# A four-layer hybrid decoder trunk on one core: wide value projection, split conditioning, transposes put later, inverse joins set apart, residual stream kept by blocks

## The chip, the core and the metric

The kernel runs on one core of a Trainium2 chip. The metric is the device time of one execution in microseconds, the median of several. TensorE (PE) multiplies matrices, and its weight loads (PEld) overlap its matmuls; VectorE (DVE), ScalarE (ACT) and GpSimd (POOL) work elementwise; SyncE (SP) here only issues DMAs. Each engine runs its instructions in a fixed order.

## What is computed

Four layers work on x of 1024 positions by 1024 features in float32. Each is a norm, a conditioning (shift, scale and gate from a vector c), an input projection, a mixer, a SiLU gate, an output projection and a gated residual add:

```python
for i in range(4):
    mod = c @ ada_w[i] + ada_b[i]                 # 1024 x 3072
    shift, scale, gate = split(mod, 3)
    h = rmsnorm(x, norm_g[i]) * (1 + scale) + shift
    y = (hgrn2, swa, gdn)[i % 3](h)               # layers 0 and 3: hgrn2
    x = x + gate * y
```

- HGRN2 (layers 0 and 3), 8 heads of 128: q, f, values i and gate z are h @ w_in. A gated linear recurrence runs in its chunked form; its output is normed per head, multiplied by silu(z) and projected.
- Attention with a sliding window of 128 (layer 1), 16 query heads, 4 key/value heads, rotary embedding, norms of q and k, learned sinks.
- Gated DeltaNet (layer 2), 8 q/k heads and 16 value heads of 128: a convolution of 4 taps over q, k and v, decays per head, chunks solved with a triangular inverse.

## The kernel before, in words

**Tiles.** x and h are held transposed, features on the 128 partitions. The 1024 positions are two halves of 512 (`hf` 0 and 1); a half is 8 blocks of 128 features. A product in float32 precision is three matmuls in a faster form (`mm3`, L204 to L206): both factors are split into a rounded part `hi` and the rest `lo`, and hi·hi, hi·lo and lo·hi are added. So a weight is loaded as `w_raw` (SP), rounded by ScalarE (`w_hi`, L179) and subtracted by VectorE (`w_lo`, L180). There are three buffers of `raw` and four of each split part.

**Projections.** `proj_fm` (L508) keeps 128 columns of weights in the array and streams 512 positions, for each half 8 blocks x 3 matmuls; then an `evac` function takes the sum from PSUM. `proj_tm` keeps activations in the array and streams 256 columns of weights: the values of HGRN2 (two heads at a time) and q, k and v of the attention layer are made so.

**Start.** `load_x` (L293) transposes a half of x on TensorE. `ada_first` (L389) makes the first four of the six conditioning parts (512 columns each; parts 0 and 1 are the shift, 2 and 3 the scale): 8 matmuls of one row per part on TensorE (L400), and its columns through L449. The norm (`norm_stats`, L467; `norm_apply`, L496) follows, per block of 128 features n_t on VectorE (L504), hhi on ScalarE (L505), hlo on VectorE (L506).

**Conditioning of later layers.** `ada` multiplies on VectorE (L413), one step per block of weights, in pieces that are handed out beside the heads (`take(side, ns)`, `NS` steps per head).

**Weaving.** `weave` interleaves streams of instructions by their estimated costs: beside a head's mixing (`mix`, or `scan` and `inverse` in DeltaNet) go the projections of the next head and the conditioning. A scheduler then fixes each engine's order by priorities; `burst` and `tied` raise the priority of a group of matmuls and keep it together.

**HGRN2's head** (`mix`, L1025). Three steps of levels (1, 3, 5) make the products inside blocks of 2, 8 and 32 positions and, in the last, between the four blocks of 32 of a chunk of 128 (L1087, `lev_ps`, the 32-step). POOL copies the diagonal blocks (L1081). Chunk by chunk come the output `o_ps` and the state. The output is normed (L1132), transposed on TensorE (L1136, `ot_ps`), multiplied by the gate `zs` and stored to `od`; the last head's stays in SBUF.

**DeltaNet.** `conv` (L637) evacuates a projection and runs three steps on VectorE (L650) and two on ScalarE. Its result is transposed on TensorE at once (`trans`, L654: `ktr_ps`, `qtr_ps`, `vtr_ps`). `inverse` solves 16 chunks of 128 positions for two heads; its last part joins blocks of 32 by four small groups of matmuls (`z_ps`, L811 to L836). `ZL` says beside which head the gate projections `proj_z` stand.

**Residual stream.** After each layer x is updated in SBUF block by block (L534, L1216). Its two tiles are needed by the mixers of layers 1 and 2, so there x is stored to `xd` (`spill_x`, one DMA of 2 MB per half) and read back (`fill_x`, the same) ahead of the output projection. In the HGRN2 layers x stays in SBUF.

## Time and profile before

| what | value |
|---|---|
| three runs, us | 2686.42, 2691.14, 2692.78; median 2691.14 |
| profiled execution, its own time | 2695.95 us |
| its span, first to last instruction | 2694.2 us |
| mean granted TensorE clock | 0.992 |
| TensorE, VectorE, ScalarE, POOL busy | 97%, 75%, 47%, 5% |
| moved by DMA | 273.29 MB, mean 101 GB/s |
| chain that ended last: PE, DVE, DMA, ACT | 71%, 17%, 5%, 3% |

The page's groups give a line, an engine, an operation, output<-inputs, the shape, a count, the busy time in us and the mean ns of one, and behind the bar the idle time of the engine ahead of them with what ended it. A row of the timeline gives a start, a duration, the instruction, a count and in brackets the idle time. A row of stretches gives busy time and count for each engine, then the granted clock, the DMA share and GB/s. The stages in the span: start to about 60 us, layer 0 to 640, attention to 1130, DeltaNet to 2130, the second HGRN2 layer to the end.

### The profile page before, as it was taken

The page shows a single profiled execution, that of the slowest core. Times are in us where ns is not written, and L with a number is a line of the kernel's source. Part 1 is how long each engine was busy: PE and PEld are TensorE (multiplying, and loading weights), DVE is VectorE, ACT ScalarE, POOL GpSimd, SP SyncE. Part 2 cuts the span into 40 slices and gives each one's busy share as a digit, 9 for nine tenths or more (in the row PEclk, how much of TensorE's full clock was granted, in tenths as well). Part 3 has the DMA queues.
Part 4 walks back from the last instruction along what each step waited for, and adds up shares of the span by engine and source line. Part 5 has one row for each costly group of instructions (what it writes and reads, how often), then busy time and mean ns, then how long its engine had stood idle before and what let it go on. Part 6 is the DMA issues. An engine that isn't in the chain of part 4 may idle for free.

```text
span 2694.2 us, 51458 instructions
## 1 busy us (share of the span) xinstructions
PE 2609.7 (97%) x18927; PEld 2102.4 (78%) x18927; DVE 2010.2 (75%) x5619; ACT 1272.9 (47%) x3268; POOL 136.7 (5%) x352
## 2 busy tenths in 40 slices
PE   8999999999999999999999999999999999999998
PEld 4878878778878777677877777777788878787877
DVE  6776766788687877777988888989876766656575
ACT  4333333444454655454556556666644433333342
POOL 0000100000000000001001101100000000000000
PEclk9999999999999999999999999999999999999999
DMA  6332222344223252333343333333584221111133
GB/s 241 92 93 84 68 79 72 110 137 157 59 87 103 75 158 91 114 98 84 102 115 99 96 105 100 94 97 82 179 254 132 71 60 37 56 51 43 49 118 115
DMA packets 361490, 273.29 MB, mean 101 GB/s; under 512 B 70499, under 2 KB 294166, under 8 KB 361238
## 3 DMA queue, kind: packets, MB, share of 16 engines
q1 hardware_dynamic: 360950, 268.96, 33.9%
q8 instruction: 149, 2.44, 0.4%
q14 instruction: 103, 0.84, 0.1%
q0 software_dynamic: 288, 1.05, 0.1%
HBM read 224.77 MB, written 45.15 MB: 100 GB/s over the span
## 4 chain that ended last, share of the span: by engine, by line
PE 71%; DVE 17%; DMA 5%; ACT 3%; issue 3%; SPq 1%; POOL 0%; DVEq 0%; ACTq 0%; POOLq 0%
PE proj_ps L206 10%; PE proj_ps L205 9%; PE proj_ps L204 9%; PE outp_ps L204 5%; PE outp_ps L205 5%; PE outp_ps L206 5%; DMA ada_w<-in_ada_w_dram 3%; PE projt_ps L204 3%; PE projt_ps L206 3%; PE projt_ps L205 3%; DVE w_lo L180 2%; DVE gd_tb L650 2%; PE pv_ps L1374 1%; DVE ada_acc L413 1%; PE w_ps L890 1%
## 5 line engine op out<-in xcount | busy, mean ns | idle before, releaser
L204 PE MATMUL proj_ps<-hhi,w_hi 128*128 128x512 f32 x1664 | 675.8, 406 | 6.1 <-ACT gd_tb L648 5.9
L206 PE MATMUL proj_ps<-hhi,w_lo 128*128 128x512 f32 x1664 | 679.9, 409 | 0.0
L205 PE MATMUL proj_ps<-hlo,w_hi 128*128 128x512 f32 x1664 | 671.2, 403 | 0.0
L204 PEld LDWEIGHTS proj_ps<-hhi,w_hi 128*128 128x128 f32 x1664 | 315.3, 190 | 59.4 <-ACT gd_tb L648 6.3
L205 PEld LDWEIGHTS proj_ps<-hlo,w_hi 128*128 128x128 f32 x1664 | 314.7, 189 | 59.0 <-issue 2.4
L206 PEld LDWEIGHTS proj_ps<-hhi,w_lo 128*128 128x128 f32 x1664 | 315.0, 189 | 56.1 <-issue 1.0
L179 ACT CAST w_hi<-w_raw 128x512 fp32r<-128x512 f32 x332 | 202.0, 611 | 303.3 <-PE proj_ps L205 188.1
L180 DVE TENSOR_TENSOR w_lo<-w_raw,w_hi 128x512 fp32r<-128x512 f32 x332 | 223.1, 674 | 155.2 <-ACT w_hi L179 129.1
L205 PE MATMUL projt_ps<-w_lo,hhi 128*128 128x256 f32 x896 | 258.7, 291 | 4.7 <-DVE w_lo L180 4.7
L204 PE MATMUL projt_ps<-w_hi,hhi 128*128 128x256 f32 x896 | 257.8, 290 | 0.6 <-ACT w_hi L179 0.6
L206 PE MATMUL projt_ps<-w_hi,hlo 128*128 128x256 f32 x896 | 256.8, 290 | 0.0
L204 PE MATMUL outp_ps<-o_hi,w_hi 128*128 128x512 f32 x576 | 229.2, 400 | 4.7 <-ACT o_hi L1200 3.4
L205 PE MATMUL outp_ps<-o_lo,w_hi 128*128 128x512 f32 x576 | 229.4, 399 | 0.0
L206 PE MATMUL outp_ps<-o_hi,w_lo 128*128 128x512 f32 x576 | 226.8, 396 | 0.7 <-DVE w_lo L183 0.7
L205 PEld LDWEIGHTS projt_ps<-w_lo,hhi 128*128 128x128 f32 x896 | 171.1, 192 | 8.1 <-DVE w_lo L180 6.0
L204 PEld LDWEIGHTS projt_ps<-w_hi,hhi 128*128 128x128 f32 x896 | 171.1, 192 | 3.7 <-ACT w_hi L179 1.0
L206 PEld LDWEIGHTS projt_ps<-w_hi,hlo 128*128 128x128 f32 x896 | 170.8, 192 | 2.4 <-issue 1.0
L650 DVE SCALAR_TENSOR_TENSOR gd_tb<-gd_xs,taps,gd_tb 128x512 f32<-128x512 f32 x192 | 145.2, 756 | 28.3 <-ACT gd_tb L648 19.7
L182 ACT ACTIVATE w_hi<-w_raw,par 128x512 fp32r<-128x512 f32 (+1 forms) x136 | 94.3, 698 | 137.0 <-PE outp_ps L205 89.2
L204 PEld LDWEIGHTS outp_ps<-o_hi,w_hi 128*128 128x128 f32 x576 | 108.8, 189 | 29.1 <-ACT o_hi L1200 4.9
L413 DVE SCALAR_TENSOR_TENSOR ada_acc<-ada_w,par,ada_acc 128x512 f32<-128x512 f32 x140 | 104.8, 749 | 33.4 <-DMA ada_w<-in_ada_w_dram 32.5
L206 PEld LDWEIGHTS outp_ps<-o_hi,w_lo 128*128 128x128 f32 x576 | 108.7, 189 | 23.5 <-DVE w_lo L183 1.3
(398 smaller groups left out, 4894.8 us busy)
## 6 DMA issues: line engine op xcount, KB each, us to landing
ada_w<-in_ada_w_dram SPq DMA_DIRECT2D x160, 256.0 KB, 2.8
w_raw<-in_hg_in_w_dram SPq DMA_DIRECT2D x136, 256.0 KB, 2.8
w_raw<-in_gd_in_w_dram SPq DMA_DIRECT2D x108, 256.0 KB, 3.0
o_in<-od SPq DMA_DIRECT2D x72, 256.0 KB, 3.2
w_raw<-in_gd_out_w_dram SPq DMA_DIRECT2D x64, 256.0 KB, 2.9
w_raw<-in_sw_in_w_dram SPq DMA_DIRECT2D x48, 256.0 KB, 2.9
w_raw<-in_hg_out_w_dram SPq DMA_DIRECT2D x40, 256.0 KB, 2.8
ada_w<-in_ada_w_dram SPq DMA_DIRECT2D x8, 1024.0 KB, 9.2
```

Of the source, the lines that this page charges most:

```text
L179: nc.scalar.copy(hi, raw)
L180: nc.vector.tensor_tensor(lo, raw, hi.bitcast(F32), ALU.subtract)
L182: nc.scalar.activation(hi, raw, AF.Copy, scale=scale)
L204: mm(out, a[0], b[0], start=start, stop=False)
L205: mm(out, a[0], b[1], start=False, stop=False)
L206: mm(out, a[1], b[0], start=False, stop=stop)
L413: self.nc.vector.scalar_tensor_tensor(acc, w, c, acc, ALU.mult, ALU.add)
L650: nc.vector.scalar_tensor_tensor(y, xs[:, j:j + HT], w(j), y, ALU.mult, ALU.add)
L890: nc.tensor.matmul(po[:, hd[a]], dd["u"][a, hf][:, cs], rhs, start=True, stop=True)
L1374: nc.tensor.matmul(po[a * 64:(a + 1) * 64], vg[:, n + 1 - nkb + b, :], p4[:, :, a, :], start=b == 0, stop=b == nkb - 1)
```

## The change

- **Wide values.** HGRN2's values are made four heads at a time: 512 columns of weights are streamed, eight split weights are held, four of them in buffers of the layer (`load_wide`, `proj_wide`). Values of heads 0 to 6 of a half live in a tile of x, so x is stored and read back in these layers too; head 7 has tiles of its own.
- **Split conditioning, shift on VectorE.** The four first parts are requested at once, the second half of x after them. Parts 2 and 3 (scale) go through TensorE, parts 0 and 1 (shift) through VectorE. After parts 2 and 0 the first four blocks are normed, after 3 and 1 the others. The rotary tables move beside layer 0's heads, and `NS` is 11 for the HGRN2 layers.
- **Output of HGRN2.** For heads 0 to 6 VectorE transposes blocks of 32x32, four DMAs store them to `pd` with the blocks in their places, and during the next half head the whole is read back, multiplied by the gate and stored to `od` (`gate`). The 32-step runs as four groups of columns. The diagonal copies are on ScalarE.
- **Later transposes.** In DeltaNet `evac` may return a function that `proj_fm` runs in the middle of the next sum (`turns`).
- **Joins apart.** The four groups of joins are put behind the last projection matmul then issued (`apart`), and the inverse has a higher estimated cost.
- **Norm in pieces.** The second half's norm of a layer is handed to the next layer (`self.last`); in DeltaNet four blocks are normed behind each convolution, while eight projections of the first half run.
- **Residual by blocks.** Each finished block of x is stored from POOL's queue (`keep_x`) and read back ahead of its use in `out_mm`.
- **Gates handed out anew.** DeltaNet's gate projections stand half by half (`ZL`), HGRN2's one head later.
- **Attention** starts with values and half of q, makes all keys in one pass, and ties a block's four products with the values.

```diff
-NS = 8, 16, 10
-ZL = ((2, 0, 1),), ((3, 0, 1),), ((4, 0, 1),), ((5, 0, 1),), ((6, 0),), ((6, 1),), ((7, 0, 1),), ()
+NS = 11, 16, 10
+ZL = ((2, 1), (3, 0)), ((3, 1),), ((4, 0),), ((4, 1), (5, 0)), ((5, 1),), ((6, 0),), ((6, 1), (7, 0, 1)), ()
...
+    def keep_x(self, hf, j):
+        if self.more:
+            x, d = self.block(hf, j)
+            self.nc.gpsimd.dma_start(d, x)
...
+    def apart(self, mms):
+        with self.tc.issue_after(self.mm.ins):
+            self.tied(mms)
...
+    def load_wide(self, w, c0, pool):
+        return [self.load_w(w[:, k, c0:c0 + HT], None, (None, pool)[k % 2]) for k in range(KT)]
...
     def ada_step(self, acc, w, k):
...
-            self.nc.vector.scalar_tensor_tensor(acc, w, c, acc, ALU.mult, ALU.add)
+            self.step = self.nc.vector.scalar_tensor_tensor(acc, w, c, acc, ALU.mult, ALU.add)
...
         for k in range(KT):
-            t = self.np.tile([P, HT], F32, name="n_t", tag="n_t", bufs=NB["n_t"])
+            t = self.psum("lev", "n_t", 2)
...
+            yield 1
...
     def proj_fm(self, w, c0, evac, halves=(0, 1)):
...
+                if k == 3:
+                    self.turns()
             with self.tc.high_priority(offset=self.pe):
-                evac(hf, ps)
+                self.turn = evac(hf, ps)
...
             for j in (2, 1, 0):
-                nc.vector.scalar_tensor_tensor(y, xs[:, j:j + HT], w(j), y, ALU.mult, ALU.add)
+                last = nc.vector.scalar_tensor_tensor(y, xs[:, j:j + HT], w(j), y, ALU.mult, ALU.add)
+            self.piece = None
+            with self.tc.issue_after(last.ins):
+                drain(take(self.last, self.parts))
+            self.hold = self.piece
...
-        self.early(proj_kq(0, ds[0], ((0,),)), EV)
-        self.spill_x(1)
+        self.parts = 4
+        self.early(chain(proj_kq(0, ds[0], ((0,),)), proj_z(1, ds[1], (0,)), proj_z(2, ds[2], (0,))), EV)
+        drain(self.last)
...
+        def proj_v(m):
+            def ev(tt, ps):
+                hf, c = divmod(tt, NC)
+                if vs[hf] is None:
+                    vs[hf] = self.xslot("hg_v").rearrange("p (c a) n -> p c (a n)", a=2)
+                n = HT - m * P
+                nc.scalar.copy(vs[hf][:, c, m * HT:m * HT + n], ps[:, :n])
+                if m:
+                    nc.scalar.copy(v7[hf][:, c, :], ps[:, n:])
+            yield from self.proj_wide(self.load_wide(w_in, 2 * D + m * HT, mp), ev, range(2 * NC))
...
+        def gate():
+            h, hf, z = pend.pop()
+            rows = (slice(h * P, (h + 1) * P), slice(hf * HT, (hf + 1) * HT))
+            t = tl("tmp")
+            nc.sync.dma_start(t, self.pd[rows])
+            nc.vector.tensor_tensor(v4(z, "c b"), v4(t, "b c"), v4(z, "c b"), ALU.mult)
+            nc.sync.dma_start(od[rows], z)
...
-                            nc.gpsimd.tensor_copy(at[gs, :, gs], A[gs].rearrange("p (c t) -> p c t", c=NC))
+                            nc.scalar.copy(at[gs, :, gs], A[gs].rearrange("p (c t) -> p c t", c=NC))
...
+                        self.tied([lambda c=c, m=m: mm(c, *m) for c in range(NC) for m in (
+                            (0, 3, slice(6, 7), slice(3, 4)), (0, 0, slice(0, 4, 3), slice(1, 3)),
+                            (1, 1, slice(1, 5, 3), slice(2, 4)), (2, 2, slice(2, 3), slice(3, 4)))])
...
                 if h < HA:
-                    nc.sync.dma_start(od[h * P:(h + 1) * P, hf * HT:(hf + 1) * HT], of)
+                    nc.vector.tensor_tensor(v4(on, "b c"), v4(po, "c b"), r[:, :, None, None].to_broadcast([P, NC, 4, 32]), ALU.mult)
+                    ob = tl("tmp")
+                    nc.vector.transpose(ob, on)
...
+                    for a in range(4):
+                        nc.sync.dma_start(dst[a], ob[a * 32:(a + 1) * 32].rearrange("q (b t) -> q b t", b=4))
+                    pend.append((h, hf, d["zs", hf]))
...
+            gs = {0: [(0, "z")], 1: [], H - 2: [(h, "z"), (h + 1, "qfz")]}.get(h, [(h, "z")])
+            if h < H - 2:
+                gs.append((h + 1, "qfz" if h == 0 else "qf"))
...
+            if (hf, j) in self.due:
+                self.due.remove((hf, j))
+                self.nc.sync.dma_start(*self.block(hf, j))
...
+        self.early(chain(proj_v(0), proj_q(0, ds[0], (0, 1))))
+        drain(proj_v(1))
+        drain(self.proj_tm(self.load_tm(w_in, 1024), ev_k))
+        drain(chain(proj_z(0, ds[0]), proj_q(0, ds[0], (2, 3))))
...
+        for part, bank, col in ((2, ("lev", "ada_row", 2), 0), (0, None, D), (3, ("s", "ada_row", 1), None), (1, None, None)):
```

Three places show how the order of instructions moves. First TensorE's order at the start, before (`ada_row` is a conditioning part, the number its weight tile; `ada_ps` its columns, `x_ps` transposes of x, `proj_ps` the first projections):

```order
L400 MATMUL ada_row<-ada_w_362,par 1x512 x7
L400 MATMUL ada_row<-ada_w_383,par 1x512
L449 MATMUL ada_ps<-ones,ada_acc 128x1 x4
L400 MATMUL ada_row<-ada_w_383,par 1x512 x7
L310 MATMUL x_ps<-ident,x_in 128x128 x9
L449 MATMUL ada_ps<-ones,ada_acc 128x1 x4
L310 MATMUL x_ps<-ident,x_in 128x128 x23
L265 MATMUL taps_ps<-ident,taps_in 128x128
L204 MATMUL proj_ps<-hhi,w_hi 128x512
```

And TensorE's order there now:

```order
L331 MATMUL x_ps<-ident,x_in 128x128 x32
L433 MATMUL ada_row<-ada_w_150,par 1x512 x3
L526 MATMUL n_rb<-n_sq,ones 128x512
L433 MATMUL ada_row<-ada_w_150,par 1x512 x5
L485 MATMUL ada_ps<-ones,ada_acc 128x1 x4
L433 MATMUL ada_row<-ada_w_182,par 1x512
L485 MATMUL ada_ps<-ones,ada_acc 128x1 x4
L433 MATMUL ada_row<-ada_w_182,par 1x512
L223 MATMUL proj_ps<-hhi,w_hi 128x512
```

The first projections stood behind all four parts and both halves of x; now 24 of them stand behind part 2, the columns of parts 2 and 0 and two matmuls of part 3, ahead of the second half of x.

Second, VectorE's order at DeltaNet's start, before (`n_t` and `hlo` are the norm of the second half, `gd_tb` the convolution of the first):

```order
L504 SCALAR_TENSOR_TENSOR n_t<-x_11280,gcol,n_rb 128x512 x2
L180 TENSOR_TENSOR w_lo<-w_raw,w_hi 128x512
L506 SCALAR_TENSOR_TENSOR hlo<-n_t,mod,hhi 128x512 x2
L504 SCALAR_TENSOR_TENSOR n_t<-x_11280,gcol,n_rb 128x512 x2
L180 TENSOR_TENSOR w_lo<-w_raw,w_hi 128x512
L506 SCALAR_TENSOR_TENSOR hlo<-n_t,mod,hhi 128x512 x2
L650 SCALAR_TENSOR_TENSOR gd_tb<-gd_xs,taps,gd_tb 128x512 x2
L556 TENSOR_TENSOR gd_wab<-w_raw,gd_wab 128x8x32
L650 SCALAR_TENSOR_TENSOR gd_tb<-gd_xs,taps,gd_tb 128x512
```

And VectorE's order there now:

```order
L695 SCALAR_TENSOR_TENSOR gd_tb<-gd_xs,taps,gd_tb 128x512
L600 TENSOR_TENSOR gd_wab<-w_raw,gd_wab 128x8x32
L695 SCALAR_TENSOR_TENSOR gd_tb<-gd_xs,taps,gd_tb 128x512
L195 TENSOR_TENSOR w_lo<-w_raw,w_hi 128x512
L695 SCALAR_TENSOR_TENSOR gd_tb<-gd_xs,taps,gd_tb 128x512
L538 SCALAR_TENSOR_TENSOR n_t<-x_11000,gcol,n_rb 128x512 x2
L702 SCALAR_TENSOR_TENSOR gd_k<-gd_tb 128x512
L540 SCALAR_TENSOR_TENSOR hlo<-n_t,mod,hhi 128x512 x2
```

The convolution of k stood behind the whole norm of the second half; now the norm's pieces stand behind its three steps.

Third, SP's order in layer 0, before (`ada_w` is conditioning, `od` the outputs of a head):

```order
L177 DMA w_raw<-in_hg_in_w_dram 128x4x128 x2
L427 DMA ada_w<-in_ada_w_dram 128x512 x3
L1141 DMA od_76<-hg_tmp 128x512
L427 DMA ada_w<-in_ada_w_dram 128x512 x2
L177 DMA w_raw<-in_hg_in_w_dram 128x4x128 x2
```

And SP's order there now:

```order
L463 DMA ada_w<-in_ada_w_dram 128x512
L1221 DMA pd<-hg_tmp 32x4x128 x4
L463 DMA ada_w<-in_ada_w_dram 128x512 x3
L1100 DMA hg_tmp<-pd 128x512
L463 DMA ada_w<-in_ada_w_dram 128x512
L192 DMA w_raw<-in_hg_in_w_dram 128x4x128 x2
L1102 DMA od_76<-hg_zs 128x512
L463 DMA ada_w<-in_ada_w_dram 128x512 x3
```

One store became four stores, a read-back and a store, with loads of conditioning and weights between them.

421 lines of the change are left out of this document (240 added, 181 removed).

## The prediction

> **What bounds the kernel now.** I read the busy shares first, then the stretches by stage, then TensorE's groups and what ended its idle time.
>
> ```profile
> PE 2609.7 (97%) x18927; PEld 2102.4 (78%) x18927; DVE 2010.2 (75%) x5619; ACT 1272.9 (47%) x3268; POOL 136.7 (5%) x352
> 60.00:530.00 470.00, 456.73 (x4266) 377.91 (x4266) 330.99 (x1042) 168.25 (x398) 30.81 (x65) 0.99 0.29 85
> 1140.00:1930.00 790.00, 768.66 (x5359) 613.09 (x5357) 670.39 (x1883) 471.56 (x1471) 65.69 (x161) 0.99 0.38 100
> 2130.00:2580.00 450.00, 445.46 (x4241) 372.47 (x4241) 286.95 (x968) 163.71 (x389) 29.10 (x64) 1.00 0.16 48
> ```
>
> The stretches are the first HGRN2 layer, DeltaNet's body and the second HGRN2 layer; the columns are length, then PE, PEld, DVE, ACT, POOL, clock, DMA share, GB/s. TensorE works in 97% of the span and is idle for 2694.2 - 2609.7 = 84.5 us. So the time falls by what the change takes off TensorE's own list, plus idle time that it closes; work added to VectorE or ScalarE costs only where TensorE comes to wait for it. VectorE is the next limit: 670.4 of 790 us in DeltaNet's body.
>
> A matmul's recorded duration overlaps the next one, so I price by start-to-start distances on TensorE's timeline (start, duration):
>
> ```profile
> 66.88 0.39 PE L205 MATMUL proj_ps<-hlo,w_hi 128*128 128x512 f32 x1
> 67.10 0.39 PE L206 MATMUL proj_ps<-hhi,w_lo 128*128 128x512 f32 x1
> 67.33 0.28 PE L204 MATMUL projt_ps<-w_hi,hhi 128*128 128x256 f32 x1
> 67.44 0.28 PE L205 MATMUL projt_ps<-w_lo,hhi 128*128 128x256 f32 x1
> 67.56 0.28 PE L206 MATMUL projt_ps<-w_hi,hlo 128*128 128x256 f32 x1
> 67.68 0.28 PE L204 MATMUL projt_ps<-w_hi,hhi 128*128 128x256 f32 x1
> ```
>
> 512 columns take 0.228 us, 256 take 0.12.
>
> **The change part by part.** Durations are of the profiled execution: span 2694.2, its own time 2695.95 us, 4.8 above the median 2691.1.
>
> *Wide values.* Per HGRN2 layer 768 matmuls of 256 columns become 384 of 512. Both layers: 1536 x 0.12 = 184 against 768 x 0.228 = 175: -9 us. The Trainium skill (TensorE: Matmul & The Clock Gate, "Wait — 56ns, not 53.3ns?") gives N/2.4 ns plus about 2.5 ns for a warm matmul; by that the pairing saves 768 x 2.5 ns = 2 us instead of 9, an estimate from that page. The rows' difference, 2 x 0.12 - 0.228 = 0.012 us, is larger than the page's, and I keep it. Eight split weights are now held through a whole pass, so the next projection's weights get buffers only as the last token tile runs; no row shows this. At each of four passes it costs between nothing and two splits on VectorE (0.69 each, below): 0 to 5 us, taken +2.
>
> *HGRN2 outputs shifted by 32x32 blocks on VectorE.* For seven of eight heads the TensorE transposes go.
>
> ```profile
> 303.48 0.60 PE L1136 MATMUL ot_ps<-ident,hg_tmp 128*128 128x128 f32 x4
> 303.91 0.39 PE L1114 MATMUL o_ps<-hg_S,hg_qf 128*128 128x128 f32 x2
> L1136 PE MATMUL ot_ps<-ident,hg_tmp 128*128 128x128 f32 x128 | 20.8, 280 | 5.9 <-DVE hg_tmp L1132 5.6
> L859 DVE STREAM_TRANSPOSE gd_of<-gd_of 128x512 f32<-128x512 f32 x32 | 22.5, 704 | 0.1
> L1081 POOL COPY hg_at<-hg_A 32x128 f32<-32x128 f32 x128 | 59.9, 468 | 940.3 <-DVE hg_F L1093 556.9 <-DVE hg_A L1076 360.9 <-DVE hg_F L1098 16.8
> ```
>
> Four take 303.91 - 303.48 = 0.43 us, so 28 groups 12.0 us; with 28/32 of the 5.6 us that TensorE waited for their input, -17 us. In their place stand 28 VectorE transposes (0.70 each in DeltaNet's row), a store in four pieces, a read-back and a later gate product. Nothing on TensorE waits for these but the final projection. The 128 copies of the diagonal blocks go from POOL to ScalarE: even at POOL's 0.47 that is 30 us a layer, and ScalarE has worked 168.3 of 470: 0; if its queue is in the way, one copy for each of 32 steps, 15 us.
>
> *The 32-step of the levels.* It now runs 32 records in four column groups, the widest 64, instead of 24 in three with the widest 96.
>
> ```profile
> 157.34 0.85 PE L1087 MATMUL lev_ps<-hg_X,hg_kg 128*32 128x96 f32 x24
> 158.12 0.50 PE L206 MATMUL proj_ps<-hhi,w_lo 128*128 128x512 f32 x1
> ```
>
> 0.78 us from start to start. If the widest group sets it, a third (0.26) goes; if the count does, nothing. 32 steps: 0 to -8, taken -6.
>
> *Start.* Two of the four conditioning parts (the shift) move from TensorE to VectorE, all four are requested ahead of the second half of x, and the first four blocks are normed as soon as parts 2 and 0 are there.
>
> ```profile
> 3.05 1.37 SPq L304 DMA_DIRECT2D x_in<-in_x_dram  x3
> 40.00:45.00 5.00, 5.00 (x18) 1.63 (x17) 2.10 (x5) 0.57 (x1) 0.00 (x0) 1.00 1.07 387
> 42.97 6.17 PE L400 MATMUL ada_row<-ada_w,par 128*1 128x512 f32 x14
> 55.11 0.50 PE L204 MATMUL proj_ps<-hhi,w_hi 128*128 128x512 f32 x1
> L413 DVE SCALAR_TENSOR_TENSOR ada_acc<-ada_w,par,ada_acc 128x512 f32<-128x512 f32 x140 | 104.8, 749 | 33.4 <-DMA ada_w<-in_ada_w_dram 32.5
> L504 DVE SCALAR_TENSOR_TENSOR n_t<-x,gcol,n_rb 128x512 f32<-128x512 f32 x64 | 45.1, 742 | 2.7 <-PE n_rb L493 2.5
> L506 DVE SCALAR_TENSOR_TENSOR hlo<-n_t,mod,hhi 128x512 fp32r<-128x512 f32 x64 | 45.9, 746 | 1.4 <-ACT hhi L505 0.8
> L180 DVE TENSOR_TENSOR w_lo<-w_raw,w_hi 128x512 fp32r<-128x512 f32 x316 | 216.8, 687 | 155.1 <-ACT w_hi L179 129.1 <-PE proj_ps L206 23.4 <-ACT gd_tb L651 0.7
> ```
>
> Before, conditioning keeps TensorE until 49, and the first 48 projections run from 55.1 to 67.3. After, 11 MB (x's half 2, conditioning 8, weights 1) must land, from 3.1 us at about 0.36 MB/us (below the 387 GB/s of that row, since it ramps up): 34 us. Then half of part 1 on VectorE, 4 x 0.75 = 3, its columns about 1, four blocks of 0.742 + 0.746 = 6, and what is queued between, five splits of 0.69 and the second half's root, 5: the 48th projection ends near 50 to 53 instead of 67.3. -14 us; if VectorE's queue is twice as long -7, if it isn't in the way -19.
>
> *Norm of the second half in pieces, more hf-0 work at DeltaNet's start.* TensorE, then VectorE:
>
> ```profile
> 1131.06 0.39 PE L206 MATMUL proj_ps<-hhi,w_lo 128*128 128x512 f32 x1
> 1137.31 0.80 PE L204 MATMUL proj_ps<-hhi,w_hi 128*128 128x512 f32 x1 [5.86 <-ACT gd_tb L648]
> 1137.90 0.63 PE L205 MATMUL proj_ps<-hlo,w_hi 128*128 128x512 f32 x1
> 1138.33 0.63 PE L206 MATMUL proj_ps<-hhi,w_lo 128*128 128x512 f32 x1
> 1135.96 1.41 DVE L506 SCALAR_TENSOR_TENSOR hlo<-n_t,mod,hhi 128x512 fp32r<-128x512 f32 x2
> 1137.36 1.69 DVE L650 SCALAR_TENSOR_TENSOR gd_tb<-gd_xs,taps,gd_tb 128x512 f32<-128x512 f32 x2
> ```
>
> TensorE stood 5.9 us because the convolution on VectorE queued behind all 16 steps of the norm and its buffers didn't come free; after it matmuls are 0.43 apart, not 0.23, some 10 of them: 2 us more. The convolution now stands ahead of the norm's pieces: -8 us (-3 if half of it returns).
>
> *Waits of the mixed stages.*
>
> ```profile
> 524.69 0.63 PE L1104 MATMUL kh_ps<-ident,hg_kg 128*128 128x128 f32 x4 [1.49 <-DVE mod L439]
> L205 PE MATMUL projt_ps<-w_lo,hhi 128*128 128x256 f32 x896 | 258.7, 291 | 4.7 <-DVE w_lo L180 4.7
> L658 PE MATMUL vtr_ps<-ident,gd_tb 128*128 128x128 f32 x128 | 20.5, 279 | 1.5 <-DVE gd_tb L652 1.4
> L658 PE MATMUL ktr_ps<-ident,gd_k 128*128 128x128 f32 x64 | 10.5, 289 | 1.4 <-DVE gd_k L652 1.3
> L828 PE MATMUL z_ps<-gd_Z,gd_uq 64*64 64x64 f32 x256 | 10.3, 232 | 6.6 <-DVE gd_uq L823 6.6
> ```
>
> The conditioning of layer 1 no longer drains at the HGRN2 layer's end (11 steps a head, not 8): -2. The attention layer opens with values and half of q, not keys and values: of its 4.7 us -3. DeltaNet's transposes stand half a projection later: 1.5 + 1.4 and as much in waits hidden under modelled ends, -4. The joins are spread, but on TensorE's order only one step gets more cover: of 6.6 us -2. Tying attention's last products changes no count: 0, between -2 and +2.
>
> *What is added.* An eighth of the first stretch stands for a head: VectorE 331.0/8 = 41 us, TensorE 456.7/8 = 57, of which four projections of 48 matmuls take 44 and the head itself 13. In layer 0 VectorE now gets 11 conditioning steps a head instead of 8, 3 x 0.75 = 2.2 us, and two transposes, 1.4, and loses two splits, 1.4: 43 us. But heads 2 to 5 carry only three projections, 33 + 13 = 46 us of TensorE; the work that they lack stands in heads 0 and 1. VectorE is at 94% in these four. If it lost nothing elsewhere 0, if each head falls 4 us behind +15; taken +6. DeltaNet's gates in halves load and split 20 more weights, 20 x 0.69 = 14 us of VectorE: hidden while TensorE's 768.7 of 790 leads, +14 if not; taken 0. Eight stores and loads of 256 KB per half of x replace one of 2 MB, in all layers now: the stores on POOL's queue, ahead of DeltaNet's first memsets, which nothing needs before the first convolution; the loads on SP, each behind its block's weights and needed only when the block's 21 to 24 matmuls (5 us) have run. Taken 0; where one comes late, 2.8 us (its landing, below).
>
> Sum: -9 + 2 - 17 - 6 - 14 - 8 - 2 - 3 - 4 - 2 + 6 = -57. Profiled 2695.95 - 57 = 2639; by the median, 4.8 lower, **2634 us**.
>
> **The rivals.**
>
> *VectorE decides.* For it: 85% in DeltaNet, 94% in layer 0's middle heads. Against it: TensorE's largest idle entries are queues on VectorE, not its load. Layer 0 then costs 9 more, DeltaNet's -6 becomes +14, the attention layer's 3 are lost: 32 more, 2666 us.
>
> *Waits close further.* Of the 84.5 us idle the sum closes about 22. If half of the other 60 goes with the new order and the +6 doesn't come: 36 less, 2598 us. Against it: most is scattered in pieces under 1 us with causes the change doesn't touch.
>
> *The read-back blocks SP (slower).* SP issues in order; the read-back of `pd` waits for its four stores, the store of the gated block for VectorE, and weights queue behind both.
>
> ```profile
> od<-gd_of SPq DMA_DIRECT2D x128, 64.0 KB, 1.8
> w_raw<-in_hg_in_w_dram SPq DMA_DIRECT2D x136, 256.0 KB, 2.8
> xd<-x SPq DMA_DIRECT2D x4, 2048.0 KB, 8.0
> SPq L177 <- DVE w_lo L180: 570.3, 153, 27.3
> ```
>
> Store 1.8, read-back 2.8 and product 0.69 block up to 5.3 us at each of 28 gates, 148 us; uncovered in full, 2634 + 148 = 2782. Beyond 57/28 = 2.0 us of stall a gate the change is slower. Against it: other requests stand between store and read-back, a weight tile feeds 24 matmuls (5.5 us) and three are loaded ahead, and SP's own longest wait, 570 us, is for VectorE to free such a tile: it has time. The Trainium skill (DMA: Bandwidth & Descriptors, "Bandwidth") advises batches of 1 MiB and calls transfers under 64 KB dominated by their descriptors; that speaks against the 64 KB stores and the split of x. The rows agree in part, 256 KB in 2.8 us against 2048 KB in 8.0, but DMA is 16 to 38% busy in these stages.
>
> *It does nothing.* Given-back time of about 57 us anywhere leaves 2691.
>
> **How the numbers follow.** A measurement here tells 0.3% (8 us) from no change. Forecast, 2610 to 2658: 0.50. Waits close further, 2580 to 2610: 0.17. VectorE decides, 2658 to 2683: 0.20. No change, 2683 to 2699: 0.05. SP blocked, above: 0.08. Faster 0.50 + 0.17 + 0.20 = 0.87. The range 2590 to 2685 leaves out the last two cases and a third of the second, under 0.2.
>
> **What would show it.** Right: wide matmuls 0.228 apart, no output transposes for seven heads, the first 48 projections done by 53 us, no gap over 2 us at DeltaNet's start, TensorE over 97.5% busy, idle below 65 us. VectorE decides: TensorE's idle time in heads 2 to 5 of layer 0 ends on VectorE. SP blocked: ScalarE's weight casts wait for loads in the HGRN2 layers. Wrong altogether: the second HGRN2 layer, where nothing else moves, isn't some 15 us shorter.

## The result, and the profile after

The changed kernel takes 2669.2 us (median of 4 runs, 2666.3 to 2670.2), the kernel before, run beside it on the same chip, 2690.1 (2686.4 to 2692.8). The ratio is 0.9918, 95% interval 0.9905 to 0.9930: faster by 0.8%, 21 us, where 57 were forecast. The profiled execution took 2670.17 us (span 2668.5), 25.8 less than that of before. The line of busy shares says in short what went wrong:

```profile
PE 2573.6 (96%) x18271; PEld 2052.9 (77%) x18271; DVE 2021.2 (76%) x5655; ACT 1322.4 (50%) x3467; POOL 108.6 (4%) x278
```

TensorE's busy time fell by 2609.7 - 2573.6 = 36 us, but its idle time rose from 84.5 to 2668.5 - 2573.6 = 94.9 us; it was to fall by 22. The span and mean granted clock, first of before, then of after:

```profile
core 0: 2694.2 us, clock 0.992
```
```profile
core 0: 2668.5 us, clock 0.986
```

In the clock's records of all profiles here the granted share is 1 or 0.5 and nothing between, so the share that is missing, doubled, is time at half clock: some 0.016 x 2694 = 43 us before and 0.028 x 2669 = 75 us after.

Where this happens is seen by stages. Each row of the next two views is one: the start up to the 48th projection matmul, layer 0 up to its first output projection, then attention's output stage, DeltaNet with its outputs, and layer 3. Columns as in the prediction's stretches. Before:

```profile
0.00:67.50 67.50, 58.24 (x218) 28.48 (x219) 41.22 (x135) 31.16 (x53) 4.43 (x44) 0.97 0.68 241
67.50:526.50 459.00, 445.74 (x4226) 369.51 (x4225) 321.83 (x1023) 162.55 (x391) 30.81 (x65) 1.00 0.29 85
...
985.40:1112.20 126.80, 123.41 (x625) 91.49 (x624) 99.29 (x238) 75.40 (x174) 1.31 (x4) 0.99 0.33 98
1112.20:2120.40 1008.20, 980.23 (x6294) 785.26 (x6293) 835.40 (x2181) 573.87 (x1665) 69.23 (x171) 0.99 0.42 117
2120.40:2582.20 461.80, 455.26 (x4286) 379.73 (x4284) 295.61 (x990) 170.45 (x400) 29.37 (x64) 1.00 0.16 49
```

After:

```profile
0.00:67.30 67.30, 49.58 (x180) 29.10 (x181) 38.51 (x115) 26.13 (x45) 3.22 (x42) 0.85 0.71 256
67.30:512.30 445.00, 431.64 (x3798) 340.97 (x3796) 326.78 (x1044) 187.29 (x478) 7.25 (x8) 1.00 0.40 118
...
968.30:1104.50 136.20, 127.70 (x634) 96.59 (x633) 102.16 (x241) 75.60 (x175) 8.12 (x15) 0.95 0.34 105
1104.50:2106.10 1001.60, 975.79 (x6286) 784.86 (x6285) 838.95 (x2198) 581.67 (x1683) 78.40 (x191) 0.99 0.45 125
2106.10:2556.50 450.40, 443.17 (x3971) 350.89 (x3969) 292.69 (x1001) 188.50 (x488) 0.54 (x1) 1.00 0.25 75
```

| stage | forecast | measured | short by |
|---|---|---|---|
| start | -14 | -0.2 | 14 |
| layer 0 | -11 (wide -4.5 + 1, shift -8.5, 32-step -3, conditioning -2, VectorE +6) | -14.0 | -3 |
| its output stage | 0 | +1.4 | 1 |
| attention | -3 | -4.3 | -1 |
| attention's output stage | 0 | +9.4 | 9 |
| DeltaNet with outputs | -14 (-8 -4 -2) | -6.6 | 7 |
| layer 3 | -15 (wide -4.5 + 1, shift -8.5, 32-step -3) | -11.4 | 4 |
| sum | -57 | -25.7 | 31 |

Three stages hold most of the loss. In the start TensorE does less (49.6 against 58.2 us) but idles 17.7 us instead of 9.3, at a clock of 0.85. In attention's output stage the idle time goes from 3.4 to 8.5 us and the clock from 0.99 to 0.95. In DeltaNet neither is worse than before: the idle time is 25.8 us instead of 28.0.

What was forecast for the HGRN2 layers is there. Wide matmuls of the changed kernel on TensorE's timeline, 0.23 apart:

```profile
80.03 0.40 PE L225 MATMUL projw_ps<-w_hi,hlo 128*128 128x512 f32 x1
80.26 0.39 PE L223 MATMUL projw_ps<-w_hi,hhi 128*128 128x512 f32 x1
80.49 0.39 PE L224 MATMUL projw_ps<-w_lo,hhi 128*128 128x512 f32 x1
```

### The profile page after: what moved, and what is told of

The parts are those of the page before. It is cut to its first block, busy times and chain, and to the rows that moved or that the text cites. A ratio compares the mean times of both kernels' runs of the same rounds, so it can differ in the third digit from the quotient of the medians.

```text
span 2668.5 us, 50699 instructions
## 1 busy us (share of the span) xinstructions
PE 2573.6 (96%) x18271; PEld 2052.9 (77%) x18271; DVE 2021.2 (76%) x5655; ACT 1322.4 (50%) x3467; POOL 108.6 (4%) x278
## 4 chain that ended last, share of the span: by engine, by line
PE 70%; DVE 15%; DMA 5%; issue 5%; ACT 5%; SPq 1%; POOL 0%; DVEq 0%; ACTq 0%; POOLq 0%
PE proj_ps L225 9%; PE proj_ps L223 9%; PE proj_ps L224 9%; PE outp_ps L225 5%; PE outp_ps L224 5%; PE outp_ps L223 5%; PE projw_ps L224 2%; PE projw_ps L223 2%; PE projw_ps L225 2%; DVE w_lo L195 1%; DVE gd_tb L695 1%; DMA ada_w<-in_ada_w_dram 1%; PE pv_ps L1505 1%; PE projt_ps L224 1%; PE projt_ps L225 1%
## 5 line engine op out<-in xcount | busy, mean ns | idle before, releaser
L225 PEld LDWEIGHTS proj_ps<-hhi,w_lo 128*128 128x128 f32 x1664 | 315.4, 190 | 58.2 <-issue 0.4
L194 ACT CAST w_hi<-w_raw 128x512 fp32r<-128x512 f32 x352 | 214.4, 612 | 271.6 <-PE proj_ps L224 155.1
L195 DVE TENSOR_TENSOR w_lo<-w_raw,w_hi 128x512 fp32r<-128x512 f32 x352 | 236.7, 677 | 132.5 <-ACT w_hi L194 126.8
L695 DVE SCALAR_TENSOR_TENSOR gd_tb<-gd_xs,taps,gd_tb 128x512 f32<-128x512 f32 x192 | 145.1, 756 | 14.9 <-ACT gd_tb L693 11.3
L449 DVE SCALAR_TENSOR_TENSOR ada_acc<-ada_w,par,ada_acc 128x512 f32<-128x512 f32 x154 | 115.0, 747 | 23.2 <-DMA ada_w<-in_ada_w_dram 22.1
L224 PEld LDWEIGHTS outp_ps<-o_lo,w_hi 128*128 128x128 f32 x576 | 109.9, 191 | 24.6 <-DVE o_lo L1318 2.3
L198 DVE SCALAR_TENSOR_TENSOR w_lo<-w_raw,par,w_hi 128x512 fp32r<-128x512 f32 (+1 forms) x136 | 97.3, 718 | 41.3 <-ACT w_hi L197 40.0
L224 PE MATMUL projt_ps<-w_lo,hhi 128*128 128x256 f32 x384 | 110.8, 290 | 2.3 <-DVE w_lo L195 2.3
L223 PE MATMUL projt_ps<-w_hi,hhi 128*128 128x256 f32 x384 | 110.5, 290 | 1.7 <-ACT w_hi L194 1.7
L225 PE MATMUL projt_ps<-w_hi,hlo 128*128 128x256 f32 x384 | 110.7, 290 | 0.0
L223 PE MATMUL projw_ps<-w_hi,hhi 128*128 128x512 f32 x256 | 102.5, 406 | 2.3 <-DVE hg_q L1035 2.3
```

The source lines that it names most:

```text
L194: nc.scalar.copy(hi, raw)
L195: nc.vector.tensor_tensor(lo, raw, hi.bitcast(F32), ALU.subtract)
L198: nc.vector.scalar_tensor_tensor(lo, raw, scale, hi.bitcast(F32), ALU.mult, ALU.subtract)
L223: mm(out, a[0], b[0], start=start, stop=False)
L224: mm(out, a[0], b[1], start=False, stop=False)
L225: self.mm = mm(out, a[1], b[0], start=False, stop=stop)
```

## The experiments

Theory: the terms on TensorE's own list are right; the missing time is new waits at three places, each made larger by the half clock behind it. Rivals: VectorE's load decides; the 37 MB of added transfers hold up the output stages; the forecast's terms themselves are too large.

### The start

The changed kernel, TensorE:

```profile
28.53 1.86 PE L433 MATMUL ada_row<-ada_w,par 128*1 128x512 f32 x2 [4.48 <-DMA ada_w<-in_ada_w_dram]
33.03 1.87 PE L433 MATMUL ada_row<-ada_w,par 128*1 128x512 f32 x2
34.83 0.80 PE L223 MATMUL proj_ps<-hhi,w_hi 128*128 128x512 f32 x1
42.37 5.31 PE L433 MATMUL ada_row<-ada_w,par 128*1 128x512 f32 x12
55.54 1.52 PE L485 MATMUL ada_ps<-ones,ada_acc 128*128 128x1 f32 x8 [1.56 <-DVE mod L487]
72.11 0.50 PE L223 MATMUL projw_ps<-w_hi,hhi 128*128 128x512 f32 x1 [2.35 <-DVE hg_q L1035]
```

and VectorE between:

```profile
38.72 1.54 DVE L449 SCALAR_TENSOR_TENSOR ada_acc<-ada_w,par,ada_acc 128x512 f32<-128x512 f32 x2
49.38 0.17 DVE L521 TENSOR_SCALAR n_ms<-x_ssq 128x4 f32<-128x4 f32 x1 [9.12 <-ACT x_sq L337]
49.45 0.74 DVE L449 SCALAR_TENSOR_TENSOR ada_acc<-ada_w,par,ada_acc 128x512 f32<-128x512 f32 x1
```

VectorE stops in the middle of part 1: the second half's mean square stands ahead of the last five steps in its order and waits 9.1 us for ScalarE's squares. Part 1's columns (`ada_ps`) are ready at 57, not at 38 to 45.

**The mean square behind part 1.**

```diff
-        nc.vector.tensor_scalar(ms, ssq, 1.0 / D, EPS, ALU.mult, ALU.add)
+        with self.tc.issue_after(self.after.ins) if self.after else nullcontext():
+            nc.vector.tensor_scalar(ms, ssq, 1.0 / D, EPS, ALU.mult, ALU.add)
```

(`after` is part 1's last step, for the second half alone.)

> The second half's mean square on VectorE is made to issue after the last of part 1's conditioning steps; nothing else is edited. Theory (the start's missing 14 us stand in VectorE's in-order queue: its 9.1 us wait at 40 to 49 us for the second half's squares holds part 1's last five steps and the weights' splits behind it): part 1's columns done by 50 us instead of 57, the 48th projection ends at 56 to 60 instead of 67.3, the first wide matmuls run on by 66 instead of 72.1, and the whole is 5 to 9 us faster than the changed kernel (2660 to 2664). Rival (the start is bound by what has to land: 390 GB/s until 47 us, then weights): the 48th projection moves up but the wide matmuls still wait for their weights until about 71; 0 to 2 us.

2668.0 us, ratio 0.9909 (0.9892 to 0.9925): no gain. The 48th projection ends at 67.5. VectorE's row shows why:

```profile
51.33 0.69 DVE L195 TENSOR_TENSOR w_lo<-w_raw,w_hi 128x512 fp32r<-128x512 f32 x1 [10.30 <-ACT w_hi L194]
```

Now the split of a wide weight stands there and waits 10.3 us for ScalarE's cast. That cast is behind ScalarE's copy of part 3's row, in the changed kernel:

```profile
47.72 0.57 ACT L435 COPY ada_acc<-ada_row 1x512 f32<-1x512 f32 x1 [6.04 <-PE ada_row L433]
```

and this waits for the 12 `ada_row` matmuls that TensorE runs after 24 projections (42.37 above). The first form of the theory named only the last waiter of three queues.

**Part 3's row ahead of the projections.**

```diff
-            for g, at, n, ew in ((proj(0, ds[0], "qf", (0,)), self.start[0], 80, EW), (take(gv, 16), self.start[1], 0, 50)):
+            for g, at, n, ew in ((proj(0, ds[0], "qf", (0,)), self.start[0], 30, EW), (take(gv, 16), self.start[1], 0, 50)):
```

> One number of the changed kernel: the first projections are given the place of 30 instructions before the end of the start instead of 80. In the written order part 3's twelve remaining conditioning matmuls then stand ahead of the 24 projections on TensorE, and part 1's eight steps stand together on VectorE. Theory, in its second form (the start's missing 14 us: TensorE takes 24 projections first, so part 3's row ends at 47.7; ScalarE's copy of it holds the squares and the casts behind it, and VectorE's split and part 1 wait for these casts): part 1's columns by 47 us instead of 57, the 48th projection ends at 57 to 61 instead of 67.3, the wide matmuls run on by 62 to 67 instead of 72.1, the whole 5 to 9 us less than the changed kernel's 2669. Rival (landing of x, conditioning and weights sets it): the wide matmuls run on no earlier than 70, 0 to 3 us.

The 48th projection ends at 60.4, the wide matmuls run on at 66.0, both as expected; part 1's columns come at 51, not by 47. TensorE, and the stretch up to the 48th projection:

```profile
33.02 9.05 PE L433 MATMUL ada_row<-ada_w,par 128*1 128x512 f32 x14
50.10 0.95 PE L485 MATMUL ada_ps<-ones,ada_acc 128*128 128x1 f32 x8
66.00 0.68 PE L223 MATMUL projw_ps<-w_hi,hhi 128*128 128x512 f32 x1 [2.56 <-ACT w_hi L194]
```
```profile
0.00:60.40 60.40, 45.70 (x169) 24.83 (x170) 38.57 (x114) 24.20 (x42) 3.27 (x42) 0.89 0.78 282
```

The 7 us are there at the end of layer 0 too (612.1 against 618.8), but the whole is 2668.3 (0.9910, 0.9894 to 0.9926): the profiled execution gave 1.7 and 2.1 back in attention and its outputs and 3.5 in DeltaNet. The theory holds for the start; that the whole follows did not come true with this edit alone. Some of these differences are no more than scatter: attention's body, with one and the same program, took 347 to 353 us in the kernels of this document.

**The second half of x ahead of parts 3 and 1**, with 30: `fetch_x(1, x1)` stands before part 3's load.

> As the run with 30 instead of 80, and the second half of x is requested ahead of conditioning parts 3 and 1 instead of behind them. Theory (after the order is mended, the start is a chain behind the last transfers: x's second half, then its squares, transposes and casts on ScalarE): the second half's work fills the waiting for parts 3 and 1, the wide matmuls run on by 58 to 62 us instead of 66, 4 to 7 us more. Rival (parts 3 and 1 are what the chain waits for): they land 5 us later, the wide matmuls run on at 66 to 70, 0 to 4 us slower than with 30 alone.

The wide matmuls run on at 66.03, as without it and not at the theory's 58 to 62; the rival's loss against the run with 30 did not come either. The 48th projection ends at 61.0. What ends the wait there is the cast of a wide weight on ScalarE. The whole, 2663.9 (0.9892, 0.9875 to 0.9909), is 5 under the changed kernel and 4 under the run with 30; that difference is DeltaNet's (999.8 us instead of 1005.1, see below), not the start's. Why the casts come no earlier was not tried.

### Attention's output stage

TensorE and VectorE of the changed kernel:

```profile
1047.14 0.39 PE L224 MATMUL outp_ps<-o_lo,w_hi 128*128 128x512 f32 x1
1050.16 0.27 PE L1476 MATMUL s_ps<-band,identb 128*128 128x256 bf16 x1 [2.62 <-DVE hlo L540]
```
```profile
1049.37 0.74 DVE L540 SCALAR_TENSOR_TENSOR hlo<-n_t,mod,hhi 128x512 fp32r<-128x512 f32 x1
```

The scores `s_ps` of the last heads wait for a step of the next layer's norm, which ends at 1050.11. The two share nothing but two PSUM banks: the change keeps the norm's `n_t` under the tag `lev`, and all tiles of one tag take turns in the same buffers; the scores use it too.

**`n_t` back in SBUF, at this place only** (in two buffers).

```diff
-            t = self.psum("lev", "n_t", 2)
+            t = self.psum("lev", "n_t", 2) if hf or i != 2 else self.np.tile([P, HT], F32, name="n_t", tag="n_t", bufs=NB["n_t"])
```

> At attention's end alone, the norm's temporary of the first half is back in SBUF instead of the two PSUM banks that the scores use. Theory (attention's output stage lost 9.4 us because the norm of the first half and the scores of the last heads share these two banks): the 2.6 us wait of the scores behind the norm's last step at 1050 us is gone, no half clock of 10 us at 1084, the stage takes 128 to 131 us instead of 136.2, the whole 4 to 8 us less (2661 to 2665). Rival (the tied value products make the last heads' chain longer): the stage stays at 134 to 137, the whole within 2 us.

2657.6 us (0.9875, 0.9858 to 0.9893), 11.6 below the changed kernel. The wait is gone and the stage is back at 128, with 3.3 us of idle time instead of 8.5 and a clock of 0.98 instead of 0.95:

```profile
969.70:1097.80 128.10, 124.79 (x634) 95.23 (x633) 101.56 (x241) 75.38 (x175) 8.15 (x15) 0.98 0.36 111
```

In all 11 kernels with the shared banks, the changed one among them, this stage took 136 to 138 us, in the four with `n_t` in SBUF 128.0 to 128.5. All the added transfers are still there, so they do not cost this stage its 9 us. DeltaNet was 6.5 us shorter as well, which this edit cannot explain; it is taken up below.

**The value products untied** (each block's two products behind its own transpose, as before).

> The attention's value products stand again behind each block's own transpose, not tied together at the end. Theory (shared PSUM banks cost the stage): the output stage stays above 133 us, the attention's body is 2 to 4 us longer since the products interleave with 512-column matmuls again, the whole 0 to +4 us. Rival (the tied products make the last heads' chain longer): the output stage takes 127 to 130 us, the whole is 2 to 6 us less.

2672.4 us (0.9917, 0.9899 to 0.9934). The stage takes 138.0, which refutes the rival. Attention's body takes 351.7 instead of 349.5, as the theory expected, but that lies within the 347 to 353 us of kernels in which nothing in it was edited, so a gain from the tying is not shown.

**The residual as 2 MB transfers** (`keep_x` stores a half after its last block, `fill_x` reads it back whole).

> The residual is stored as one 2 MB transfer after each half's last gate step and read back as one, on SyncE's queue, instead of in eight blocks. Theory (the blocks cost nothing, their transfers are covered): within 2 us in every output stage and in sum within 3 us. Rival (the block transfers, 28 more issues among the weights and on GpSimd's queue, delay the output stages): the stages of layer 0, attention and DeltaNet are each 2 to 4 us shorter, the whole 5 us or more less. Third possibility, the blocks were worth their while: the whole is 4 to 10 us slower, since a 2 MB read-back takes 8 us to land and a 2 MB store holds the next half's values.

2671.1 us (0.9919, 0.9901 to 0.9936). Layer 0's output stage takes 109.3 instead of 106.5 us, attention's 136.3, DeltaNet with outputs 1001.1: the blocks cost nothing, and gain 3 us at one place at most. With attention's stage mended while all transfers stayed, the rival of the added transfers falls there; in layer 0, whose x is stored and read back only now, the output stage is 1.4 us longer than before, and no run took that transfer out alone.

### DeltaNet

**The joins as before** (no order behind the last projection matmul, former yields, 28000).

> DeltaNet's four joins back as before: each without the order behind the last projection matmul, with the former yields and the former cost of 28000. Theory (spreading the joins costs DeltaNet's body some of the 10 us that it is behind the forecast: the state's products wait longer, ks and S groups +5 us): the body is 3 to 6 us shorter, the whole as much. Rival (the forecast: the spread covers one step more): the joins' idle time rises by 2 us or more, the whole +2 to +6.

2666.9 us (0.9910, 0.9895 to 0.9924): the whole hardly differs. In the profiled run the body is 6 us shorter (644.0 from the first to the last product of k with k, instead of 650.3) and DeltaNet 998.0 instead of 1001.6, as the theory expected, but not for its reason. The waits of TensorE (us in total, times, longest) show that the forecast's saving is real; "issue" means that the profile shows nothing that the engine waited for. Changed kernel, then with the joins back:

```profile
PE z_ps L886 <- DVE gd_uq L881: 4.1, 3, 1.6
...
PE z_ps L878 <- issue: 1.7, 1, 1.7
PE z_ps L877 <- issue: 1.7, 1, 1.7
```
```profile
PE z_ps L885 <- DVE gd_uq L880: 7.3, 7, 1.7
```

Setting the joins apart takes 3.2 us of waits away, and two "issue" waits of 1.7 us take them back. With the joins back these two are gone, and so is most of the half clock (10.2 us in DeltaNet instead of 23.9, which is 7 us of time).

**The transposes at once again** (`turns` called right behind the evacuation).

> In DeltaNet the transposes of a projection's result stand right behind its convolution again, not half a projection later. Theory (the forecast's 4 us): their idle time on TensorE rises to 4 to 8 us from 5.6, the whole +3 to +5. Rival (the transposes' results come later now and the scan waits for them, part of the 10 us that DeltaNet's body is behind the forecast): the whole 2 to 5 us less.

2673.1 us (0.9926, 0.9909 to 0.9943), DeltaNet 1006.4 instead of 1001.6: 4.8 more. But 3.4 of that is half clock (DeltaNet's granted clock makes 30.7 us at half instead of 23.9), and TensorE's waits for the convolutions' results are alike, 5.5 and 5.6 us, against 4.0 before the change. If the half clock is not the edit's doing, at most 1.4 us is left for it: the forecast's 4 are not confirmed, and neither is the loss.

**The two "issue" waits.** Between the first and the last product of k with k, the changed kernel and nine of the others have the same 4514 matmuls and 4513 weight loads in the same order, but for a few small products whose records change places; these stretches took 641 to 657 us. The changed kernel, the run with 30, and the run with HGRN2's transposes on TensorE (below), each over just this stretch (length first, clock third from the end):

```profile
1167.93:1818.19 650.26, 631.59 (x4514) 508.31 (x4513) 579.46 (x1643) 405.16 (x1271) 59.64 (x147) 0.99 0.40 104
```
```profile
1164.81:1821.86 657.05, 633.90 (x4514) 508.74 (x4513) 578.77 (x1643) 404.70 (x1271) 60.28 (x147) 0.99 0.40 103
```
```profile
1187.59:1828.70 641.11, 624.46 (x4514) 502.10 (x4513) 579.08 (x1643) 404.98 (x1271) 60.19 (x147) 1.00 0.41 106
```

The longer ones have a wait inside a burst of joins and half clock right behind it; the third has neither. The changed kernel, TensorE's row, stretches around it (the clock is the third number from the end), and the instruction queue in the 1.2 us from 1435.5 on (transfers, MB, share of 16 engines):

```profile
1437.92 0.18 PE L878 MATMUL z_ps<-gd_Uc,gd_Z 32*32 32x32 f32 x1 [1.68 <-issue]
```
```profile
1434.00:1438.30 4.30, 2.62 (x101) 2.04 (x102) 3.54 (x6) 1.25 (x2) 3.57 (x7) 1.00 0.34 114
1438.30:1441.70 3.40, 3.40 (x29) 2.65 (x31) 3.09 (x5) 2.52 (x7) 0.00 (x0) 0.51 0.36 84
1441.70:1446.00 4.30, 4.30 (x60) 3.48 (x58) 3.24 (x6) 3.65 (x10) 0.10 (x1) 0.99 0.00 0
```
```profile
q8 instruction: 1, 0.02, 5.0%
```

The page counts this queue's transfers over the whole execution:

```profile
q8 instruction: 144, 2.36, 0.4%
```

That is 16.4 KB each, and the trace has 36,926 records of TensorE (36,542 matmuls and weight loads and 384 others, almost all waits on semaphores): one transfer for 256 of them. The kernel before has 38,256 and 149 transfers, again one for 256. Counted from the start, the two waits stand at records 19,393 and 20,673, both 193 past a multiple of 256, and some 0.6 us before each began, such a transfer had started. So TensorE seems to run out of instructions: a transfer takes some 2.3 us until its instructions run, and the joins' small products pass 256 records in some 3 us. If so, moving the program by some instructions must move the waits.

The other profiles bear this out. In the 16 of this document TensorE has 25 "issue" waits of over 0.1 us; all are in DeltaNet, and each stands 193 or 194 past a multiple of 256. The 16 of over 1 us all end 2.2 to 2.4 us after such a transfer began. But the place alone does not make the wait: in the run with `n_t` in SBUF the same two places cost 0.12 and 0.24 us, which fits its shorter DeltaNet, and with 30 they cost 1.68 and 1.95. Why a transfer starts early enough in one run and not in another is not shown.

**40 useless matmuls in the start** (128 columns, in TensorE's wait at 24 to 28 us, behind part 2's columns; all else as changed).

```diff
+    def warm(self, n):
+        ps = self.proj_ps("warm_ps")
+        with self.tc.issue_after(self.cols.ins):
+            for _ in range(n):
+                self.nc.tensor.matmul(ps[:, :P], self.ident, self.ident, start=True, stop=True)
...
+                    k.warm(40)
```

> The changed kernel with 40 more matmuls of 128 columns on TensorE in its wait for part 3 at 24 to 28 us; their result is never read. Theory for DeltaNet's stalls (the two waits of 1.7 us within the joins' bursts, put down to nothing by the profile, stand at TensorE's instruction 193 of a block of 256, 0.6 us after a 16 KB transfer on the instruction queue began): the added matmuls move the blocks' ends by some 80 instructions, out of the joins' bursts; both waits and the half-clock stretches right behind them go, DeltaNet's body takes 640 to 646 us instead of 650. Rival (they come from the joins themselves): both waits stay within 0.5 us. In the start: if half clock costs it, the first 24 projections take 5.5 to 6 us instead of 7.6 and the stretch at half clock from 26 to 40 us is gone or shorter, 1 to 4 us; otherwise no change.

Both waits are gone, the stretch takes 646.4, and the kernel with 40 matmuls more is 9 us faster than the changed one: 2659.9 (0.9878, 0.9859 to 0.9897); in the profiled run DeltaNet is 5.4 us shorter. The shift was larger than expected: each of these float32 matmuls runs as two, with a weight load each, so the blocks move by some 160 records and not by 80. In the start the 24 projections took 5.7 instead of 7.6 us, but the added ones held TensorE until 33 instead of 28.5; the 48th projection came 1.0 us earlier.

**Both mends together** (30, and `n_t` in SBUF).

> Both mends together: the first projections placed 30 instructions before the end of the start, and the norm's temporary of attention's first half in SBUF. Theory (both causes are real and independent): the start keeps its 7 us, attention's output stage its 7, the whole 2654 to 2658 when DeltaNet's body (650.3 us in the changed kernel's profiled run, first to last product of k with k) stays as it is, 2648 to 2654 when its two stalls of 1.7 us stay away. Rival (what is gained early is given back in DeltaNet, as in the run with 30 alone): 2657 or more, no better than the second mend alone.

2650.2 us, ratio 0.9844 (0.9827 to 0.9862): faster than both kernels, 19 us below the changed one. The 48th projection ends at 59.0, attention's output stage takes 128.0. The two joins' waits are still there (1.89 and 1.70 us), and the body takes 653.5 us, so the theory asked for 2654 to 2658: its two gains came, and the whole is 4 us lower than they explain (2653.5 in the profiled execution, the longest of four).

**This kernel with 20, and with 55, useless matmuls** of 32 columns.

> The run with both mends, and 20 matmuls of 32 columns more in TensorE's wait at 24 to 28 us; their result is never read. Theory (the joins' stalls come where the end of a block of 256 TensorE instructions falls into them): by the order and times of the run with both mends, a shift of 80 instructions leaves no block that TensorE passes in under 4.8 us, so no stall of over 0.5 us put down to nothing, DeltaNet's body 641 to 647 us instead of 653.5, the whole 2641 to 2647 instead of 2650. Rival (the stalls of the padded run went by chance, or by the start's clock): one or both stay, 2648 to 2653.

> The same with 55 such matmuls instead of 20. Theory: a shift of 220 instructions puts block ends into five of DeltaNet's joins (five blocks of under 4 us, the shortest 3.0): three to five stalls of 1 to 2 us, most with half clock behind them, DeltaNet's body 652 to 662 us, the whole 2650 to 2660. Rival (only the added matmuls' presence counts, not their number): the same body and whole as with 20, within 3 us.

With 20 there is no "issue" wait over 0.1 us, with 55 there are five; four of these (the fifth is 0.13), two of them at the product right behind a burst of joins, and then the stretches with 20 and with 55:

```profile
1259.67 0.21 PE L884 MATMUL z_ps<-gd_Uc,gd_Z 32*32 32x32 f32 x1 [0.87 <-issue]
1346.09 0.21 PE L885 MATMUL z_ps<-gd_Z,gd_Uc 32*32 32x32 f32 x1 [1.82 <-issue]
1440.02 0.33 PE L714 MATMUL vtr_ps<-ident,gd_tb 128*128 128x128 f32 x1 [1.49 <-issue]
1532.69 0.40 PE L224 MATMUL proj_ps<-hlo,w_hi 128*128 128x512 f32 x1 [1.23 <-issue]
```
```profile
1152.68:1798.16 645.48, 627.95 (x4514) 502.39 (x4513) 578.43 (x1643) 406.39 (x1274) 57.61 (x147) 1.00 0.40 105
```
```profile
1167.54:1821.52 653.98, 634.01 (x4515) 507.28 (x4514) 578.28 (x1643) 406.33 (x1274) 57.40 (x147) 0.99 0.40 103
```

All five stand 193 or 194 past a multiple of 256; half clock follows within 2 us behind two of them (1346.09 and 1440.02), not behind most. The scheduler gave the padded kernels an order of their own in this stretch, but these two have the same one, so that the number of added matmuls alone tells them apart. The theory holds for DeltaNet. For the whole it didn't: 20 gave 2652.6 (0.9856, 0.9838 to 0.9874), no better than none, since the matmuls took 7.7 us, most of it at half clock, and moved the 48th projection from 59.0 to 61.1; 55 took 22.7 us there and moved it to 77.6, and their 2669.6 (0.9924, 0.9909 to 0.9938) is that loss.

### The terms of the HGRN2 layers

**Values in matmuls of 256 columns again** (each sum made in two halves of columns; weights, order and evacuations stay).

> The values' matmuls of both HGRN2 layers are 256 columns wide again, two for each one of 512; their order, weights and evacuations stay. Forecast's term: 1536 x 0.12 - 768 x 0.228 = +9 us. By the stages' accounts (the groups took 93.6 and 92.7 us instead of 98.7 and 99.5) it is +12. If TensorE's time for them were hidden behind VectorE in these stages (rival: VectorE decides), 0 to +4.

2678.7 us (0.9949, 0.9934 to 0.9964), 9.5 more; layer 0 is 6.3 and layer 3 4.0 us longer. So the term is some 10 us. The Trainium skill's price (TensorE: Matmul & The Clock Gate, "Wait — 56ns, not 53.3ns?") gives an estimate of 2 us for the pairing: these matmuls don't agree with it.

**All heads' outputs transposed on TensorE and gated at once**, as before.

> All HGRN2 heads' outputs are transposed on TensorE and gated at once, as before; no store and read-back, no later gate product. The forecast's term says +17 us. By TensorE's distances in the changed kernel (2 x 6.0 us of output transposes gone from the two layers, the idle time in front of them shown elsewhere) it is +10 to +14. Rival (VectorE decides: its 28 transposes and gates' waits took back what TensorE gained): 0 to +6.

2683.1 us (0.9968, 0.9958 to 0.9978), 13.9 more. The profiled execution, 6 us above that median, says more of the layers themselves: layer 0 is 14.9 and layer 3 9.6 us longer, 24.5 together, while DeltaNet, untouched, is 9.8 us shorter (991.8): here it has no "issue" wait, and 6.8 us at half clock instead of 23.9. TensorE's idle time ahead of these transposes is back:

```profile
L1220 PE MATMUL ot_ps<-ident,hg_tmp 128*128 128x128 f32 x112 | 17.6, 280 | 7.8 <-DVE hg_tmp L1216 7.4
```

**The 32-step** was not undone by itself, but the trace of the changed kernel gives its price, from the start of its 32 matmuls to the next product:

```profile
94.79 0.65 PE L1164 MATMUL lev_ps<-hg_X,hg_kg 128*32 128x32 f32 x32
95.37 0.50 PE L224 MATMUL projw_ps<-w_lo,hhi 128*128 128x512 f32 x1
```

It takes 0.58 us instead of 0.78, in 31 of the 32 steps alike: 6.4 us for all 32.

## Why the prediction was too high

- **Wide values, -9 + 2:** right: 10 us by undoing. That run kept the eight held weights, so the hand-over's 2 us is not in it; but outside the start no wait of TensorE for a weight's split or cast shows up in the HGRN2 layers.
- **Shift on VectorE, -17:** too small; undoing it costs 24.5 us in the two layers of the profiled execution. **32-step, -6:** right, 6.4.
- **VectorE's +6 in layer 0:** did not come. The rival "VectorE decides" is refuted with it: TensorE's idle time in layer 0 was 459.00 - 445.74 = 13.3 us and is 445.00 - 431.64 = 13.4, of which 2.35 belong to the start (at 72.11, above) and 3.13 to a new wait at the layer's end, of which the forecast had no term:

```profile
512.25 0.50 PE L223 MATMUL outp_ps<-o_hi,w_hi 128*128 128x512 f32 x1 [3.13 <-ACT o_hi L1317]
```

  Before, the first output projection of layer 0 did not wait; ScalarE casts an output here that SP requested only at 508.21, behind three weight tiles. All 15 kernels with the change have this wait (2.7 to 3.7 us), the one without the later gate too. Inside the heads TensorE thus waits less than before. That the measured 2669 lies beside this rival's 2666 is chance.
- **Start, -14: the step that failed.** It said that after the landing only "five splits of 0.69 and the second half's root, 5" are queued between, and put the 48th projection at 50 to 53. It came at 67.3. The working added durations on VectorE and left out that two other engines' orders lie in the same chain: 24 projections ahead of part 3's row on TensorE, its copy ahead of the casts on ScalarE, these ahead of part 1 on VectorE. With the first knot out it is 60.4, half of the missing 14 us. The other half is read from that run's rows and was not tried: part 1 starts at 38, not at 34, takes eight steps there and not four, and its columns wait behind projections (50.10). The clock adds to it: it is at half from 25 to 39, across and behind TensorE's wait of 4.5 us ahead of 28.53, and again from 56 to 63, which at 0.15 x 67 is 10 us of clock lost in the start, against 2 before.
- **Attention's output stage, 0: the second failure.** The forecast weighed the tied products there, which are innocent, and overlooked one line of the diff, the new home of `n_t`. Its price is 8 us.
- **DeltaNet, -8 - 4 - 2:** its start gains as forecast: the wait of 5.86 us is gone, TensorE is idle for 0.8 us instead of 9.0 up to the first product of k with k. The joins' waits fell as forecast (4.1 instead of 6.6), the transposes' did not. What took some 7 us back were the two instruction waits and the half clock behind them; in the three runs without such a wait and with the joins apart DeltaNet takes 992 to 996, 12 to 16 less than before, with -14 forecast.
- **Layer 3, -15:** -11.4. By the stretches above TensorE's busy time fell by 12.1 us, of the 13.5 that were to go from its list there (wide 4.5, output transposes 6, 32-step 3); its idle time rose from 6.5 to 7.3 instead of falling. What waits opened there was not followed up.
- **The read-back of gates on SP** costs TensorE nothing: ScalarE's casts wait for weight loads for 16.2 us in layer 0 instead of 10.1, and for 2.7 instead of 7.0 in layer 3, but TensorE waits for none of these casts. The blocks of x cost nothing either: both were taken at 0.

So the mechanism, TensorE's list as the bound, was right, and the terms on that list came out right or larger than forecast. The loss was in idle time and clock: the sum let 22 us of waits close and none open. What was to show it right did for the wide matmuls, the transposes and DeltaNet's start, and did not for the 48th projection, TensorE's share (96%) and the idle time (94.9 us).

## What to carry to other kernels

When a step is moved to another engine, follow the chain through the order of every engine that it crosses, not only through the durations on the new one: the wait that shows is the last of several. When a temporary changes its pool, list who else uses the new buffers at each place where it runs. On a kernel that TensorE bounds, read the granted clock beside every new gap: where half clock follows, a gap of 2 us can cost as much again.
